# Hybrid encoder step: feed-forward as seven block products for eight, operands made in the attention output's evacuation, rms applied behind the products

## The chip, the cores and the metric

One core of a Trainium2 chip. TensorE (PE) multiplies into PSUM, of which there are eight banks of 128 x 512 words; VectorE (DVE), ScalarE (ACT) and GpSimd (POOL) do the elementwise work, the first two with access to PSUM; SyncE (SP) issues every transfer of this kernel. The metric is the device time of one execution in microseconds, the median of the runs shown.

## What is computed

One layer of an encoder for 1024 prompt tokens and 32 sample tokens, T = 1056 in all, with 1024 features. Two token mixers, a cross-attention to 256 memory rows, then a gated feed-forward of width 2816 and a last norm. The part that the change touches:

```python
x = x + cross_attend(rmsnorm(x, lw['norm_cross']), mk, mv, lw['w_cq'], lw['w_co'])
n = rmsnorm(x, lw['norm_ffn'])
x = x + (jax.nn.silu(n @ lw['w_ff1']) * (n @ lw['w_ff3'])) @ lw['w_ff2']
...
y_prompt = rmsnorm(xp, norm_final)
```

All inputs are float32.

## The kernel before

Activations are kept feature-major: a tile of 128 features by up to 1056 tokens. Every large matrix product is done in the fast float32r form of TensorE, with each operand split into a high and a low part (a ScalarE copy to float32r, then a subtraction), and three products for one: high by high, high by low, low by high. `gemm` runs over token blocks of 352 (`BLOCKS`), for each over the k tiles of 128, with three matmuls per k tile, and hands each filled PSUM bank to an evacuation. `load_w` brings a column tile of a weight, multiplies it by a gain where one is given (VectorE), and splits it.

Nothing is issued as it is written: each call becomes a node of a graph, and `Graph.order` simulates the five engines with prices (`price`), picks for each engine the most urgent node (longest path to the end less a bias), and gives out PSUM banks and SBUF places. The order on each engine is then fixed, the queue of SP included. SBUF is cut into regions (`REGIONS`, in units of 66 words a partition, given out in pages of 16 units): f0 and wr hold float32, r0 float32r, mb and ma change their type from phase to phase. `FIFO` says how many tiles of a class may live at once. `LEAD` says how many nodes of earlier phases may be left when a phase opens.

The last stages are:

- `cross` ends with the product by `w_co`, eight column tiles in three blocks each. Its evacuation `residual` adds the product to x, which is held as its two parts `xh` and `xl`, splits the sum into them again (ScalarE, GpSimd), and gathers the squares; `rstd` makes 1/rms of every token, `rb`.
- `ffn` makes the hidden layer in 22 column tiles of 128. For each, two `gemm` calls over x (`w_ff1`, `w_ff3`, with the gain multiplied into the weights), evacuations `evac1` and `evac3` that apply `rb`, the sigmoid and the gate, and a split of the hidden values into two parts that stay in SBUF. After 6, 12, 18, 20 and 22 hidden tiles (`FF_GROUPS`) `ff2` multiplies a group by its rows of `w_ff2` and adds to eight accumulators `acc`; the residual x is added in the first two groups.
- The last group goes block by block (`LAST`), followed by `final`: transposes to token-major, the last norm, the writes.

## Time and profile before

| | |
|---|---|
| median of 3 runs | 2032.84 us (2032.03 to 2032.9) |
| the profiled execution, first to last instruction | 2034.7 us |
| TensorE, busy | 1954.2 us |
| VectorE, ScalarE, GpSimd, busy | 1101.1, 801.0, 622.5 us |
| mean granted TensorE clock | 0.978 |
| HBM read, written | 86.69, 11.55 MB |

The times in the table but the first row are of one profiled execution. The busy time of an engine is the union of its instructions' spans. PE rows are matmuls, PEld rows weight loads. In the rows of groups, a name before the arrow is what is written and one behind it what is read: `bank` is PSUM, and the other names are the regions of SBUF (r is r0; f is f0), since every instruction is issued from one line of `emit`. Shapes are partitions by elements; the numbers behind the first bar are the group's busy time in us and the mean of one instruction in ns. Lines of the timeline begin with start and length in us; the rows by stretch give busy us and instruction counts of PE, PEld, DVE, ACT and POOL.

### The profile page before, as it was taken

The page shows a single profiled execution, that of the slowest core. Times are in us where ns is not written, and L with a number is a line of the kernel's source. Part 1 is how long each engine was busy: PE and PEld are TensorE (multiplying, and loading weights), DVE is VectorE, ACT ScalarE, POOL GpSimd, SP SyncE. Part 2 cuts the span into 40 slices and gives each one's busy share as a digit, 9 for nine tenths or more (in the row PEclk, how much of TensorE's full clock was granted, in tenths as well). Part 3 has the DMA queues.
Part 4 walks back from the last instruction along what each step waited for, and adds up shares of the span by engine and source line. Part 5 has one row for each costly group of instructions (what it writes and reads, how often), then busy time and mean ns, then how long its engine had stood idle before and what let it go on. Part 6 is the DMA issues. An engine that isn't in the chain of part 4 may idle for free.

```text
span 2034.7 us, 36538 instructions
## 1 busy us (share of the span) xinstructions
PE 1954.2 (96%) x14417; PEld 1813.2 (89%) x14417; DVE 1101.1 (54%) x2584; ACT 801.0 (39%) x2066; POOL 622.5 (31%) x954
## 2 busy tenths in 40 slices
PE   7989999998999899899999999999999999999998
PEld 6878777787877788899989999999999999999997
DVE  4876677768767766635754356333333344323345
ACT  4576546845765676633332233121111112111122
POOL 4742343334434331206300056230022233310221
PEclk8999999998999999899999999999999999999999
DMA  4100100011010101541211111111211111111112
GB/s 139 42 22 25 35 23 27 23 34 33 22 32 18 33 23 58 179 147 42 73 42 42 42 53 42 42 40 40 59 50 39 40 58 42 50 40 53 46 42 86
DMA packets 159115, 100.59 MB, mean 49 GB/s; under 512 B 7776, under 2 KB 153824, under 8 KB 158944
## 3 DMA queue, kind: packets, MB, share of 16 engines
q1 hardware_dynamic: 158944, 98.26, 16.0%
q8 instruction: 113, 1.85, 0.4%
q14 instruction: 58, 0.48, 0.1%
HBM read 86.69 MB, written 11.55 MB: 48 GB/s over the span
## 4 chain that ended last, share of the span: by engine, by line
PE 59%; DVE 4%; POOL 1%; ACT 1%; issue 1%; DMA 1%; SPq 0%; DVEq 0%; ACTq 0%
PE bank L337 59%; DVE f L337 2%; ACT f L337 1%; POOL f L337 1%; DVE r L337 1%; POOL r L337 1%; DVE mb L337 0%; ACT mb L337 0%; DMA wr<-in_w_ck_dram 0%; ACT r L337 0%; DMA f<-mix_scratch 0%; DMA wr<-in_w_cq_dram 0%; DVE wr L337 0%; SPq L337 0%; POOL mb L337 0%
## 5 line engine op out<-in xcount | busy, mean ns | idle before, releaser
L337 PE MATMUL bank<-r 128*128 128x352 f32 x5904 | 1040.1, 331 | 12.4 <-POOL r L337 5.3
L337 PEld LDWEIGHTS bank<-r 128*128 128x128 f32 x5904 | 955.1, 190 | 27.6 <-POOL r L337 5.8
L337 DVE TENSOR_TENSOR f<-bank,f 128x256 f16<-128x256 f32 (+9 forms) x689 | 252.6, 391 | 355.4 <-PE bank L337 339.8
L337 PE MATMUL bank<-mb,r 128*128 128x352 f32 (+3 forms) x2448 | 411.5, 325 | 4.6 <-DVE r L337 2.5
L337 PEld LDWEIGHTS bank<-mb,r 128*128 128x128 f32 x2448 | 396.1, 188 | 9.5 <-DVE r L337 4.3
L337 POOL TENSOR_TENSOR f<-f 128x352 f32<-128x352 f32 (+6 forms) x242 | 198.2, 835 | 482.0 <-ACT f L337 459.4
L337 PE MATMUL bank<-f 128*128 128x64 f16 (+7 forms) x2612 | 291.6, 253 | 35.2 <-DVE f L337 15.7
L337 ACT CAST r<-wr 128x1024 fp32r<-128x1024 f32 (+2 forms) x154 | 145.1, 946 | 311.8 <-PE bank L337 298.1
L337 ACT ACTIVATE f<-f 128x256 f32<-128x256 f32 (+5 forms) x372 | 147.0, 411 | 245.9 <-DVE f L337 217.7
L337 PEld LDWEIGHTS bank<-f 128*128 128x128 f32 (+4 forms) x1564 | 163.6, 162 | 66.8 <-DVE f L337 16.9
L337 ACT COPY f<-f 64x256 f16<-64x256 f16 (+1 forms) x408 | 149.1, 367 | 46.1 <-DVE f L337 37.8
L337 DVE TENSOR_TENSOR r<-wr,r 128x1024 fp32r<-128x1024 f32 (+2 forms) x124 | 142.1, 1150 | 43.5 <-ACT r L337 43.3
L337 DVE TENSOR_TENSOR wr<-wr,f 128x1024 f32<-128x1024 f32 x82 | 105.8, 1292 | 104.5 <-DMA wr<-in_w_ff_dram 89.1
L337 POOL TENSOR_TENSOR r<-f,r 128x352 fp32r<-128x352 f32 x48 | 62.3, 1312 | 271.1 <-DVE f L337 216.9
L337 POOL TENSOR_SCALAR f<-f 128x64 f32<-128x64 f32 (+6 forms) x124 | 54.7, 442 | 159.2 <-DVE f L337 100.0
L337 DVE TENSOR_TENSOR ma<-bank,ma 128x352 f32<-128x352 f32 (+6 forms) x96 | 45.3, 486 | 94.6 <-PE bank L337 84.1
L337 PEld LDWEIGHTS <-f 128*128 128x128 f16 x1156 | 52.5, 99 | 35.6 <-issue 8.2
L337 POOL TENSOR_TENSOR r<-wr,r 128x1024 fp32r<-128x1024 f32 x30 | 71.7, 2393 | 29.5 <-ACT r L337 25.9
L337 ACT CAST mb<-f 128x352 fp32r<-128x352 f32 x66 | 30.9, 484 | 123.0 <-DVE f L337 114.7
L337 PE MATMUL bank<-f,mb 64*64 64x64 f32 (+7 forms) x830 | 75.3, 250 | 1.4 <-DVE f L337 1.1
L337 ACT ACTIVATE f<-bank,f 128x256 f32<-128x256 f32 (+4 forms) x122 | 51.1, 432 | 56.4 <-DVE f L337 19.7
L337 DVE TENSOR_TENSOR f<-bank,r 128x352 f32<-128x352 f32 x60 | 30.4, 518 | 77.0 <-PE bank L337 77.0
(167 smaller groups left out, 1770.6 us busy)
## 6 DMA issues: line engine op xcount, KB each, us to landing
wr<-in_w_ff_dram SPq DMA_DIRECT2D x44, 512.0 KB
wr<-in_w_in_dram SPq DMA_DIRECT2D x30, 512.0 KB
wr<-in_w_ff_dram SPq DMA_DIRECT2D x24, 384.0 KB
f<-mix_scratch SPq DMA_DIRECT2D x24, 176.0 KB
mb<-in_x_prompt_dram SPq DMA_DIRECT2D x16, 256.0 KB
wr<-in_w_ck_dram SPq DMA_DIRECT2D x8, 512.0 KB
wr<-in_w_cv_dram SPq DMA_DIRECT2D x8, 512.0 KB
wr<-in_w_out_dram SPq DMA_DIRECT2D x8, 512.0 KB
```

Source lines behind the costliest of these rows:

```text
L337: getattr(eng, method)(*args, **kw)
```

## The change

The feed-forward's three matrix products are done blockwise, 2 x 2 blocks on each side, with seven block products for eight (Winograd's form of Strassen's scheme). For the hidden layer a block of the weight is 512 inputs by 128 columns and a block of x 512 features by 264 tokens; the token halves are taken twice (`s` = 0, 1), each of 2 x 264 tokens. The weight's sums are made by `fast_w` from a raw tile of 256 columns as they are needed (four sums, then a high and a low part for each of seven operands). The sums of x (`operands`) are made in the evacuation of the product by `w_co`, which now runs in four blocks of 264, scales x by the norm's gain there and writes x itself to a scratch in DRAM. `xh` and `xl` then hold the operands of products 1, 2, 3 and 7; those of 5, 6 and 4 are split in `ff_hidden`. `fast` runs the seven products in a given order into four pairs of banks, three of which are used twice.

`ff_hidden` makes all 11 pairs of hidden tiles first; 1/rms is applied to both factors behind the products in tiles of 4 x 264. The hidden values and their differences are written to DRAM, and `ff_out` reads them back as operands of `w_ff2`, ten pairs in five groups of two, split anew; x is read back and added in the third group, and sums common to several output blocks are added in the last. The eleventh pair is multiplied plainly, block by block as before, with `final` behind it; `final`'s identity is made anew ahead of it. float32r weights have a region of their own, cut from r0. Elsewhere the diff removes comments.

```diff
-FF_GROUPS = (6, 6, 6, 2, 2)
+FF_GROUPS = (2, 2, 2, 2, 2)
+TQ = T // 4
...
-REGIONS = {"f0": (192, "left", "FFFFFF", ()), "wr": (32, "left", "FFFFFF", ()), "r0": (320, "left", "RRRRRR", ()),
-           "mb": (192, "left", "FRRRRR", (150,)), "ma": (64, "right", "FRRRFF", (1000, 150))}
+REGIONS = {"f0": (192, "left", "FFFFFFF", ()), "wr": (32, "left", "FFFFFFF", ()), "r0": (256, "left", "RRRRRRR", ()), "rw": (64, "left", "RRRRRRR", ()),
+           "mb": (192, "left", "FRRRRRR", (150,)), "ma": (64, "right", "FRRRFFF", (1000, 150))}
...
-LEAD = {0: BIG, 1: 1100, 2: 250, 3: 400, 4: 300, 5: 40}    # a phase opens when so many nodes of the ones before it are left
+LEAD = {0: BIG, 1: 1100, 2: 250, 3: 400, 4: 300, 5: 200, 6: 200}
...
+FIFO = {"wr": 2, "wh": 2, "wl": 2, "p": 44, "rp": 5, "op": 56, "sr": 2, "sh": 4, "sl": 4, "sx": 4, "sh3": 8, "sl3": 8, "hst2": 4, "xr": 2, "wr2": 4, "wh2": 8, "wl2": 8, "ckv": 7, "mrow": 2}
...
-            self.gemm(w, act, KD, self.residual(m, sq))
+            self.gemm(w, act, KD, self.operands(m, sq), blocks=[(TQ * q, TQ) for q in range(4)])
...
+    def operands(self, m, sq):
+        nc = self.nc
+        V, S, G = nc.vector, nc.scalar, nc.gpsimd
+        def new(name):
+            return self.ap.tile([128, TQ], F32, tag=name, name=name)
+        def evac(t0, n, ps):
+            s, h = divmod(t0 // TQ, 2)
+            hs, ls = self.xh[:, m, t0:t0 + n], self.xl[:, m, t0:t0 + n]
+            t, x, k = new("xs"), new("xg"), m % 4
+            self.x[m, s, h] = x
+            V.tensor_tensor(t, ps, hs.bitcast(F32), ALU.add)
+            V.tensor_tensor(t, t, ls.bitcast(F32), ALU.add)
+            S.activation(x, t, AF.Copy, scale=self.P("g_ffn", m))
+            nc.sync.dma_start(self.x_dram[:, m, t0:t0 + n], t)
+            if m >= 4 or h == 0:
+                self.split(hs, ls, x)
+            if m < 4 and h == 1:
+                t1 = self.t[5, k, s] = new("t1")
+                G.tensor_tensor(t1, x, self.x[k, s, 0], ALU.subtract)
+            if m >= 4 and h == 1:
+                E = V if m == 7 else G
+                t2, t3, t4 = self.t[6, k, s], _, self.t[4, k, s] = new("t2"), new("t3"), new("t4")
+                E.tensor_tensor(t3, x, self.x[k, s, 1], ALU.subtract)
+                self.split(self.xh[:, k, t0:t0 + n], self.xl[:, k, t0:t0 + n], t3)
+                E.tensor_tensor(t2, x, self.t[5, k, s], ALU.subtract)
+                E.tensor_tensor(t4, self.x[m, s, 0], t2, ALU.subtract)
+            if m == 0:
+                S.activation(sq[:, t0:t0 + n], t, AF.Square)
+            else:
+                S.activation(t, t, AF.Square)
+                G.tensor_tensor(sq[:, t0:t0 + n], sq[:, t0:t0 + n], t, ALU.add)
+        return evac
...
+    def halves(self, ap):
+        v = ap.rearrange("p (s h u) -> p s h u", s=2, h=2)
+        return v[:, :, 0], v[:, :, 1]
...
+    def fast_w(self, ap, nk, order, tags, pairs):
+        nc = self.nc
+        V, S, G = nc.vector, nc.scalar, nc.gpsimd
+        raw = self.wp.tile([128, nk, 2, 256], F32, tag="sr", name="fraw")
+        if pairs:
+            nc.sync.dma_start(raw, ap.rearrange("(k e p) m -> p k e m", e=2, p=128))
+        else:
+            for e in range(2):
+                nc.sync.dma_start(raw[:, :, e], ap[128 * nk * e:128 * nk * (e + 1)].rearrange("(k p) m -> p k m", p=128))
+        a11, a21, a12, a22 = raw[:, :, 0, 0:128], raw[:, :, 0, 128:256], raw[:, :, 1, 0:128], raw[:, :, 1, 128:256]
+        s1, s2 = (self.ap.tile([128, nk, 128], F32, tag="sx", name=t) for t in ("s1", "s2"))
+        G.tensor_tensor(s1, a21, a22, ALU.add)
+        G.tensor_tensor(s2, s1, a11, ALU.subtract)
+        for i in order:
+            if i == 7:
+                G.tensor_tensor(a21, a11, a21, ALU.subtract)
+            if i == 3:
+                G.tensor_tensor(a12, a12, s2, ALU.subtract)
+            part = {1: a11, 2: a12, 3: a12, 4: a22, 5: s1, 6: s2, 7: a21}[i]
+            hi, lo = (self.wp.tile([128, nk, 128], F32R, tag=tag, name="f" + tag[:2]) for tag in tags)
+            S.copy(hi, part)
+            V.tensor_tensor(lo, part, hi.bitcast(F32), ALU.subtract)
+            yield hi, lo
...
+    def fast(self, ws, act, nk, evac, order):
+        nc = self.nc
+        ps = {}
+        for i in order:
+            nc.bias = self.turn
+            self.turn += 0.73 * nk
+            hi, lo = next(ws)
+            bank = " aadcdbc"[i]
+            fresh = (bank, 0) not in ps
+            for s in range(2):
+                if fresh:
+                    ps[bank, s] = self.psg.tile([128, TQ], F32, tag="g", name="ps_f")
+                p = ps[bank, s]
+                for k in range(nk):
+                    if k % CUT == 0:
+                        nc.cut()
+                    ah, al = act(i, k, 0, s), act(i, k, 1, s)
+                    nc.tensor.matmul(p, lhsT=hi[:, k], rhs=ah, start=fresh and k == 0, stop=False, skip_group_check=True)
+                    nc.tensor.matmul(p, lhsT=hi[:, k], rhs=al, start=False, stop=False, skip_group_check=True)
+                    nc.tensor.matmul(p, lhsT=lo[:, k], rhs=ah, start=False, stop=k == nk - 1, skip_group_check=True)
+                evac(i, s, p)
...
+    def ff_hidden(self):
+        nc = self.nc
+        V, S, G = nc.vector, nc.scalar, nc.gpsimd
+        ops = {}
+        self.turn = 0.0
+        for n, i in enumerate((5, 6, 4)):
+            nc.bias = 3.0 * n
+            for k in range(4):
+                for s in range(2):
+                    ops[i, k, s] = [self.ap.tile([128, TQ], F32R, name=f"t{i}{p}") for p in "hl"]
+                    self.split(*ops[i, k, s], self.t[i, k, s])
+        def act(i, k, lo, s):
+            if i in (4, 5, 6):
+                return ops[i, k, s][lo]
+            t0 = TQ * (2 * s + (i in (3, 7)))
+            return (self.xl if lo else self.xh)[:, k + 4 * (i in (2, 3)), t0:t0 + TQ]
+        rb = self.rb.rearrange("p (s h u) -> p s h u", s=2, h=2)
+        dram = []
+        for m in range(DFF // 256):
+            last = m == DFF // 256 - 1
+            shape = [128, 2, T] if last else [128, 2, 7, TQ]
+            d = nc.real.dram_tensor(f"h_scratch{m}", shape, F32, kind="Internal").ap()
+            dram.append(nc.tile(shape, F32, f"h_dram{m}", fixed=d))
+            cs = slice(256 * m, 256 * m + 256)
+            order = (1, 6, 7, 5, 4, 2, 3) if m else (1, 2, 7, 5, 3, 6, 4)
+            out, u, full = [[None, None], [None, None]], [None, None], [False, False]
+            def sums(f, i, s, ps):
+                if i == 1:
+                    out[f][s] = self.ap.tile([128, 4, TQ], F32, tag="ft4", name="tv"[f])
+                    u[s] = self.ap.tile([128, TQ], F32, tag="fu", name="fu")
+                    full[s] = False
+                    S.copy(u[s], ps)
+                    return
+                o = out[f][s]
+                if i == 6:
+                    V.tensor_tensor(u[s], ps, u[s], ALU.add)
+                    full[s] = True
+                    if order[1] != 6:
+                        G.tensor_tensor(o[:, 2], o[:, 2], u[s], ALU.add)
+                        G.tensor_tensor(o[:, 3], o[:, 3], u[s], ALU.add)
+                elif i == 2:
+                    S.copy(o[:, 0], ps)
+                elif i == 5:
+                    V.tensor_tensor(o[:, 2], ps, o[:, 2], ALU.add)
+                else:
+                    dst = o[:, {7: 2, 4: 1, 3: 3}[i]]
+                    if full[s]:
+                        V.tensor_tensor(dst, ps, u[s], ALU.add)
+                    else:
+                        S.copy(dst, ps)
+            def evac1(i, s, ps):
+                sums(0, i, s, ps)
+                if i == order[-1]:
+                    t, sg = out[0][s], self.ap.tile([128, 4, TQ], F32, tag="ft4", name="sg")
+                    r = rb[:, s].unsqueeze(2).to_broadcast([128, 2, 2, TQ])
+                    th = t.rearrange("p (h a) u -> p h a u", a=2)
+                    V.tensor_tensor(th, th, r, ALU.mult)
+                    S.activation(sg, t, AF.Sigmoid)
+                    G.tensor_tensor(t, t, sg, ALU.mult)
+                    (G if s else V).tensor_tensor(th, th, r, ALU.mult)
+            def evac3(i, s, ps):
+                sums(1, i, s, ps)
+                if i == order[-1]:
+                    x, y = out[1][s], self.ap.tile([128, 4, TQ], F32, tag="ft4", name="ht")
+                    V.tensor_tensor(x, x, out[0][s], ALU.mult)
+                    if last:
+                        for b, (e, h) in enumerate(((0, 0), (1, 0), (1, 1), (0, 1))):
+                            t0 = TQ * (2 * s + h)
+                            nc.sync.dma_start(dram[m][:, e, t0:t0 + TQ], x[:, b])
+                        return
+                    G.tensor_tensor(y[:, 2], x[:, 3], x[:, 0], ALU.subtract)
+                    G.tensor_tensor(y[:, 0], x[:, 2], y[:, 2], ALU.subtract)
+                    G.tensor_tensor(y[:, 1], x[:, 2], x[:, 3], ALU.subtract)
+                    G.tensor_tensor(y[:, 3], x[:, 1], y[:, 0], ALU.subtract)
+                    nc.sync.dma_start(dram[m][:, s, 0:3], x[:, 0:3])
+                    nc.sync.dma_start(dram[m][:, s, 3:7], y)
+            for name, evac in (("w_ff1", evac1), ("w_ff3", evac3)):
+                self.fast(self.fast_w(self.i[name][0, :, cs], 4, order, ("sh", "sl"), False), act, 4, evac, order)
+        return dram
...
+    def ff_out(self, hidden):
         V, S, G = nc.vector, nc.scalar, nc.gpsimd
         fp = self.ap
+        order = (1, 6, 7, 5, 2, 4, 3)
+        acc = [fp.tile([128, T], F32, tag="ac", name="acc") for _ in range(KD)]
+        common = [fp.tile([128, 2, TQ], F32, tag="ac", name="common") for _ in range(KD // 2)]
+        def operands(ms):
+            ops = {}
+            for at, i in enumerate(order):
+                nc.bias = self.turn + 0.73 * len(ms) * at
+                for k, m in enumerate(ms):
+                    raw = fp.tile([128, 2, TQ], F32, tag="hst2", name="hraw")
+                    nc.sync.dma_start(raw, hidden[m][:, :, (0, 0, 1, 2, 6, 5, 3, 4)[i]])
+                    hi, lo = (fp.tile([128, 2, TQ], F32R, tag="op", name=t) for t in ("fh", "fl"))
+                    S.copy(hi, raw)
+                    (V if k % 2 else G).tensor_tensor(lo, raw, hi.bitcast(F32), ALU.subtract)
+                    ops[i, k] = hi, lo
+            return lambda i, k, lo, s: ops[i, k][lo][:, s]
+        def evac(g, j, i, s, ps):
+            c = [[h[:, s] for h in self.halves(acc[2 * j + e])] for e in range(2)]
+            dst = {1: common[j][:, s], 6: common[j][:, s], 2: c[0][0], 7: c[1][1], 5: c[1][1], 4: c[1][0], 3: c[0][1]}[i]
+            if g == 0 and i not in (5, 6):
+                S.copy(dst, ps)
+            else:
+                V.tensor_tensor(dst, ps, dst, ALU.add)
+            if i == order[-1] and g == len(FF_GROUPS) - 1:
+                for n, dst in enumerate((c[1][1], c[1][0], c[0][1])):
+                    (V if n == 2 else G).tensor_tensor(dst, dst, common[j][:, s], ALU.add)
+        at = 0
+        for g, n in enumerate(FF_GROUPS):
+            rows = slice(256 * at, 256 * (at + n))
+            act = operands(range(at, at + n))
+            for j in range(4):
+                w = self.fast_w(self.i["w_ff2"][0, rows, 256 * j:256 * j + 256], n, order, ("sh3", "sl3"), True)
+                self.fast(w, act, n, partial(evac, g, j), order)
+                if g == 2:
+                    for m in (2 * j, 2 * j + 1):
+                        x = fp.tile([128, T], F32, tag="xr", name="xr")
+                        nc.sync.dma_start(x, self.x_dram[:, m])
+                        G.tensor_tensor(acc[m], acc[m], x, ALU.add)
+            at += n
+        nc.phase, nc.bias = 6, self.turn
+        hs = []
+        for e in range(2):
+            raw = fp.tile([128, T], F32, tag="xr", name="hraw2")
+            nc.sync.dma_start(raw, hidden[at][:, e])
+            hs.append([fp.tile([128, T], F32R, name=t) for t in ("fh2", "fl2")])
+            self.split(*hs[e], raw, V if e else G)
+        ws = [self.load_w(self.i["w_ff2"][0, 256 * at:, 128 * m:128 * m + 128], 2, small=True) for m in range(KD)]
...
+        for b in LAST:
+            for m in range(KD):
+                def add(t0, n, ps, m=m):
+                    V.tensor_tensor(acc[m][:, t0:t0 + n], ps, acc[m][:, t0:t0 + n], ALU.add)
+                self.gemm(ws[m], lambda k, lo, t0, n: hs[k][lo][:, t0:t0 + n], 2, add, blocks=[b])
```

78 lines of the change are left out of this document (18 added, 60 removed).

## The prediction

> **What bounds the kernel now.** I read the page, then the chain of waits, then the table by stretches.
>
> ```profile
> span 2034.7 us, 36538 instructions
> ...
> PE 1954.2 (96%) x14417; PEld 1813.2 (89%) x14417; DVE 1101.1 (54%) x2584; ACT 801.0 (39%) x2066; POOL 622.5 (31%) x954
> ...
> PEclk8999999998999999899999999999999999999999
> ...
> GB/s 139 42 22 25 35 23 27 23 34 33 22 32 18 33 23 58 179 147 42 73 42 42 42 53 42 42 40 40 59 50 39 40 58 42 50 40 53 46 42 86
> ```
> ```profile
> 1254.16 0.86 PE bank L337 x2
> 1255.05 753.06 PE bank L337 x4654
> 2009.52 0.59 POOL f L337
> ```
> ```profile
> core 0: us, PE busy (x) PEld busy (x) DVE busy (x) ACT busy (x) POOL busy (x), PEclk, DMA share, GB/s
> 1160.00:1230.00 70.00, 69.65 (x429) 69.06 (x429) 27.11 (x39) 18.70 (x37) 30.76 (x27) 1.00 0.13 39
> 1230.00:1260.00 30.00, 28.93 (x169) 27.01 (x169) 23.89 (x31) 13.81 (x27) 23.21 (x18) 1.00 0.19 53
> ...
> 1400.00:1950.00 550.00, 550.00 (x3410) 550.00 (x3409) 197.75 (x288) 88.51 (x141) 124.11 (x114) 1.00 0.16 47
> ```
>
> The chain has one unbroken piece of 753 us in which nothing but TensorE decides: the feed-forward. In the 550 us stretch inside it TensorE never stops, its granted clock is 1.00, and VectorE, ScalarE and GpSimd are busy 36%, 16% and 23%. So this stage's time is the number of products times their spacing: 550 / 3410 = 161.3 ns for a moving operand of 352 columns. Fewer or narrower products are worth their full spacing here, and there is elementwise room to pay with.
>
> **What one narrower product costs.** The change uses moving operands of 264 columns; none runs in this kernel. The nearest row is the memory's keys and values, with 256 columns (timeline, then groups kept apart by shape):
>
> ```profile
> 842.00 5.87 PE L337 MATMUL bank<-r,ma 128*128 128x256 f32 x48
> ```
> ```profile
> L337 PEld LDWEIGHTS bank<-r 128*128 128x128 f32 x5904 | 955.1, 190 | 27.6 <-POOL r L337 5.8 <-ACT mb L337 3.4 <-DVE r L337 2.7
> L337 PE MATMUL bank<-r,ma 128*128 128x256 f32 x384 | 53.2, 296 | 0.9 <-DVE r L337 0.9
> L337 PEld LDWEIGHTS bank<-r,ma 128*128 128x128 f32 x384 | 49.9, 201 | 1.7 <-DVE r L337 1.1 <-ACT r L337 0.2 <-ACT f L337 0.2
> ```
>
> Forty-eight in 5.87 us, the last one's own 296 ns taken off: (5.87 - 0.296) / 47 = 118.6 ns. The line to 161.3 at 352 columns is 0.445 ns a column, so 264 columns cost 118.6 + 8 x 0.445 = 122.2 ns. A weight load lasts about 190 ns by either row, yet one passes every 118.6 ns: loads overlap, and a load's length is no floor at 122.
>
> The Trainium skill (TensorE: Matmul & The Clock Gate, Back-to-back issue gap) gives for back-to-back products one column per 2.4 GHz cycle plus 2.5 ns: 149.2 and 112.5 ns as estimates from that page, and the exchange below would then save 83 us; the trace's spacings are 8 to 9% longer, and I use those.
>
> **Products.** Removed: 22 column tiles x 8 x 3 x 3 blocks for each of two input matrices, and 20 x 8 x 3 x 3 of the output matrix: 4608 x 161.3 ns = 743.3 us (the last pair, 144 products, stays as it is). Added: 11 pairs x 2 x 7 products x 2 halves x 12 = 3696, and 5 groups x 4 x 7 x 2 x 6 = 1680: 5376 x 122.2 ns = 656.9 us. Gain 86.4 us. The attention output is re-cut from 3 blocks to 4: 768 x 122.2 - 576 x 161.3 ns = +0.9 us. Net -85.5 us on the path that sets the end.
>
> **Elementwise work, against 41.1 us of TensorE per unit** (one pair of the hidden layer or one group of the output matrix: 336 x 122.2 ns either way).
>
> ```profile
> L337 POOL TENSOR_TENSOR f<-f 128x352 f32<-128x352 f32 x96 | 104.2, 1111 | 389.8 <-ACT f L337 388.6
> L337 DVE TENSOR_TENSOR f<-bank,f 128x352 f32<-128x352 f32 x114 | 58.8, 523 | 197.6 <-PE bank L337 197.5
> L337 DVE TENSOR_TENSOR r<-wr,r 128x1024 fp32r<-128x1024 f32 x38 | 47.1, 1240 | 12.6 <-ACT r L337 12.6
> L337 DVE TENSOR_TENSOR wr<-wr,f 128x1024 f32<-128x1024 f32 x38 | 46.6, 1226 | 73.2 <-DMA wr<-in_w_ff_dram 73.1
> L337 ACT CAST r<-wr 128x1024 fp32r<-128x1024 f32 x38 | 39.6, 1043 | 51.4 <-PE bank L337 51.4
> ```
> ```profile
> L337 DVE TENSOR_TENSOR r<-wr,r 128x256 fp32r<-128x256 f32 x16 | 6.2, 422 | 0.0
> L337 ACT CAST r<-wr 128x256 fp32r<-128x256 f32 x16 | 6.0, 404 | 4.1 <-DMA wr<-in_w_ff_dram 4.0
> ```
> ```profile
> 1256.52 1.38 DVE L337 TENSOR_SCALAR f<-bank 128x352 f32<-128x352 f32 x3
> ```
> ```profile
> L337 POOL TENSOR_TENSOR r<-wr,r 128x1024 fp32r<-128x1024 f32 x30 | 71.7, 2393 | 29.5 <-ACT r L337 25.9 <-PE bank L337 3.2
> ```
>
> Three VectorE instructions of 352 columns in a row took 1.38 us, the last one about 0.52: they start every 0.43 us. With some 1.07 ns a column between 256 and 1024 columns, VectorE gives 0.32 (256), 0.33 (264), 0.60 (512), 0.62 (528) and 1.2 us (1056). ScalarE, 0.83 ns a column: 0.40, 0.41, 0.62, 0.63, 1.07. GpSimd, 1.11 to 2.39: 0.93, 0.94, 1.42, 1.45, 2.45.
>
> Hidden layer, per pair. VectorE: 14 low parts of 512, 20 sums of 264, 5 multiplies of 1056: 8.4 + 6.6 + 6.0 = 21 us. ScalarE: 14 high parts, 8 copies, 2 sigmoids: 14 us. GpSimd: 8 weight sums, 3 multiplies of 1056, 8 differences: 11.4 + 7.4 + 7.5 = 26 us. All lie beside 41.1 us of products; the 44 multiplies by the gain at about 1.23 us (the wr<-wr,f row) go away. Uncovered, each engine's excess over 41.1 would count.
>
> Output matrix, per group. VectorE: 56 sums of 264, 28 low parts of 256, 7 of 528: 18.5 + 9.0 + 4.3 = 32 us. ScalarE 20 us. GpSimd: 16 weight sums, 7 low parts: 25 us; the third group adds 8 x 2.45 us for the residual, together 44.6, over the 41.1; the last adds 16 x 0.94, together 40.
>
> Now the row that speaks against the change. Where VectorE's two inputs are both SBUF and GpSimd runs, they take turns:
>
> ```profile
> 1235.80 2.42 POOL L337 TENSOR_TENSOR f<-f 128x352 f32<-128x352 f32 x2
> ...
> 1236.14 0.51 DVE L337 TENSOR_TENSOR f<-bank,r 128x352 f32<-128x352 f32 x1
> ...
> 1236.57 2.03 DVE L337 TENSOR_TENSOR f<-f,r 128x352 f32<-128x352 f32 x2
> ...
> 1238.17 1.23 POOL L337 TENSOR_TENSOR r<-f,r 128x352 fp32r<-128x352 f32 x1
> ...
> 1238.52 1.97 DVE L337 TENSOR_TENSOR r<-wr,r 128x1024 fp32r<-128x1024 f32 x1
> ```
>
> Two 352-column adds from SBUF took 2.03 us for 0.95 alone, and a low part 1.97 for 1.24; the add with an input from PSUM, under a running GpSimd, kept its 0.51. So sums out of PSUM are free of GpSimd and the rest adds to it. Added in line, per hidden pair 14.4 + 26 = 40 of 41 us; per output group 13 + 25 = 38, in the third 58, in the last 56 with its combining adds. The first kind just fits and costs delay, not rate. For the third group the price lies between 0 (GpSimd's rows above already hold some waiting, and operands are kept two groups ahead) and 17 us; I take 8, near the middle. For the last, 0 to 15, I take 3, since its combining adds gate only the plain pair. For the other three 0 to 5, I take 1. Hidden layer: 0 to 15 over eleven pairs, I take 3. Output matrix +12, hidden +3.
>
> **Start of the feed-forward.** The 24 operands of products 5, 6 and 4 are split in a region which the attention's operands leave only when its last product has run. In the first call (20.5 us) VectorE then has 24 x 0.33 + 11 low parts x 0.6 + the rms chain and sums, some 25 us, and GpSimd is already late there (23.21 of 30 us). Between 0 (this call's order puts products 6 and 4 last) and 10 (its excess over 20.5, with GpSimd's turns); I take 4. Beside it, each of 32 blocks writes x to DRAM and ScalarE's square, in place, waits for that write; behind it stand the high parts of the next block. ScalarE is busy 18.70 of 70 us in this stage, and even 1 us more a block leaves it under the 94 us of products: nothing, and up to 32 us of ScalarE if that cover were gone.
>
> **Transfers.** The hidden values go out (48 writes) and come back (70 reads of 270 KB and 2 of 540), with 32 + 8 for x. Per output group that is 14 x 0.27 + 4 x 0.52 = 5.9 MB in 41 us, 143 GB/s, against 47 in the stretch above. The page's rate by slices reached 179, so it fits; four buffers give each read some 11 us. All go through SP's one queue, where a write waiting for VectorE holds the weight loads behind it; these are asked for a call, 20 us, ahead. Taken as nothing, kept in the range.
>
> The tail is the same plain pair and final norm, with the identity remade by GpSimd ahead of it; VectorE arrives there busier: +1 (-3 to +4).
>
> **Sum.** The profiled execution: 2034.7 - 85.5 + 3 + 12 + 4 + 1 = 1969.2 us. The runs' median is 1.9 us under that span, so 1967.
>
> **Rivals.**
> 1. All of it hides: only products count. 2034.7 - 85.5 - 1.9 = 1947, 1948 with the tail. For it: the engines' sums above are all under 41.1 but one. Against: the taking of turns. 0.20.
> 2. Taking turns decides the whole output matrix: 35 SBUF-only VectorE instructions a group each wait half a microsecond behind GpSimd, 32 + 17 = 49 us for 41; five groups lose 40, the start 8, the hidden layer 5: 1948 + 53 = 2001. For it: GpSimd's occupancy of 60% and more; against: today's low parts, at 23% GpSimd, take 1240 ns against 1226 for the same-sized multiply, hardly any waiting. 0.20. The Trainium skill (SBUF — State Buffer, Who interferes with whom) states it as an exclusive lock held for a whole instruction; by that rule the trace agrees, 2.03 us for two adds.
> 3. Narrow products don't hold their spacing, as on arrival of freshly made weights: at 138 ns, 5376 x 138 = 742, nothing is gained, the attention output costs 13 more, and with the other terms it is 2034.7 - 1 + 13 + 20 - 1.9 = 2065. Against: the 256-column row. 0.02.
> 4. Slower: room. A pair's sums live in tiles of 16 units, and if the next pair's cannot be given out until this pair's hidden values are written, TensorE stands through the last sum 0.33, multiply 1.2, four differences 3.8 and a write of about 2.7 (an estimate): 8 us x 11 = 88, 1967 + 88 = 2055. It decides from fewer than six free places; I count 16 places of 16 units less two for the raw weights, two for constants, three for weight sums and small tiles, so nine. 0.06.
> 5. My forecast, 1967, own range 1955 to 1985. 0.52.
>
> **How the numbers follow.** A measurement of this kernel tells about 0.2% (4 us) from no change. Forecast, 1 and 2 are all faster: 0.92; of the 0.08 of 3 and 4, milder forms of which end near today's time, 0.01 is put within 0.2% and 0.07 slower. The range takes in rival 1 less 3 us for a planner that orders the earlier stages anew, and rival 2: 1945 to 2004.
>
> **What would show it.** Right: 5376 products with 264 columns at 121 to 123 ns where they run in a row; a chain of TensorE through the hidden layer in 440 to 470 us; the five output groups at 205 to 230 us with gaps of TensorE released by VectorE or GpSimd in the third; low parts of the weights longer than 0.6 and 0.42 us. Wrong: spacing over 130 ns; gaps at each pair's start released by a DMA or by GpSimd; TensorE idle over 40 us in all of the feed-forward.

## The result, and the profile after

| | before | after |
|---|---|---|
| median of the runs compared, us | 2032.43 (2030.44 to 2032.9, 4 runs) | 2044.99 (2041.77 to 2047.24, 4 runs) |
| ratio | 1 | 1.0062 [1.0048, 1.0076] |
| profiled execution's span, us | 2034.7 | 2040.0 |

The change makes the kernel 0.6% slower. 1967 us was forecast, within 1945 to 2004. The page of the changed kernel, with the rows that answer to those shown of the one before:

```profile
span 2040.0 us, 40406 instructions
...
PE 1892.7 (93%) x15377; PEld 1739.6 (85%) x15377; DVE 1431.3 (70%) x3093; ACT 944.9 (46%) x2454; POOL 910.2 (45%) x1159
...
PE   7899999998998999899999997999999999899898
...
PEclk9999989999999999899999998999999999999999
...
PE 8%; DVE 3%; issue 2%; POOL 2%; DMA 1%; ACT 0%; DVEq 0%; ACTq 0%; POOLq 0%
```

TensorE's busy time fell by 61.5 us (1954.2 to 1892.7) and the span rose. The work did leave TensorE; its place was taken by idle time. The unbroken piece of 753 us of TensorE at the end of the chain is gone as well. The feed-forward's stages by stretch (columns: length, then busy us and instructions of PE, PEld, DVE, ACT, POOL, then the granted clock, the DMA share, GB/s): the product by `w_co` and the first pair, the other ten pairs, the output matrix.

```profile
1134.00:1320.00 186.00, 162.90 (x1193) 156.05 (x1192) 126.06 (x218) 80.83 (x194) 85.58 (x77) 0.94 0.20 63
1320.00:1760.00 440.00, 413.15 (x3295) 407.67 (x3294) 311.68 (x384) 126.16 (x240) 272.84 (x193) 0.98 0.30 100
1760.00:1990.00 230.00, 214.19 (x1691) 209.06 (x1691) 219.30 (x418) 100.50 (x251) 145.71 (x133) 0.99 0.44 137
```

In the hidden layer no engine but TensorE is over 71% busy, and TensorE still stands for 27 of 440 us. What ended those stops (the table of waits of that stretch: us in all, times, the longest):

```profile
PE bank L340 <- DVE ma L340: 16.6, 8, 2.9
PE bank L340 <- DVE f L340: 4.7, 2, 2.7
PE bank L340 <- ACT rw L340: 3.8, 8, 1.0
PE bank L340 <- DVE rw L340: 1.7, 8, 0.2
```

A sum of VectorE ("ma", "f") ends the large ones, about one a pair. One of them in the timeline of the changed kernel (start, length, engine, operation, how many, idle time before and who ended it):

```profile
1427.86 0.69 DVE L340 TENSOR_TENSOR rw<-ma,rw 128x512 fp32r<-128x512 f32 x1
...
1428.93 1.26 DVE L340 TENSOR_TENSOR f<-f 128x1056 f32<-128x1056 f32 x1
...
1431.43 2.80 POOL L340 TENSOR_TENSOR f<-f,ma 128x1056 f32<-128x1056 f32 x1 [6.18 <-ACT ma L340]
1431.81 5.85 DVE L340 TENSOR_TENSOR rw<-ma,rw 128x512 fp32r<-128x512 f32 x2
...
1434.18 5.81 POOL L340 TENSOR_TENSOR f<-f 128x1056 f32<-128x1056 f32 x2
...
1437.58 0.76 DVE L340 TENSOR_TENSOR f<-bank,f 128x264 f32<-128x264 f32 x2
...
1438.22 3.10 PE L340 MATMUL bank<-mb,rw 128*128 128x264 f32 x24
1438.27 2.27 DVE L340 TENSOR_TENSOR rw<-ma,rw 128x512 fp32r<-128x512 f32 x1
1439.95 1.73 POOL L340 TENSOR_TENSOR ma<-wr 128x512 f32<-128x512 f32 x1
1440.46 2.33 DVE L340 TENSOR_TENSOR f<-f 128x1056 f32<-128x1056 f32 x1
...
1442.72 0.42 DVE L340 TENSOR_TENSOR ma<-bank,f 128x264 f32<-128x264 f32 x1
...
1443.29 3.19 PE L340 MATMUL bank<-mb,rw 128*128 128x264 f32 x24 [1.97 <-DVE ma L340]
```

The first two rows show VectorE alone: 0.69 us for a low part of 512 columns, 1.26 for a multiply of 1056. GpSimd's three multiplies of the gate (2.80 and 5.81 us) then run from 1431.4 to 1440.0. Under them two low parts take 5.85 us and a third 2.27; a fourth instruction, the multiply, takes 2.33 under GpSimd's weight sum. The sums out of a bank keep about 0.4 us each. VectorE does its queue in order, so the sum at 1442.72, whose bank the next product needs, stands behind them, and TensorE waits 1.97 us. This comes back at the same product of every pair: ten stops of 2.2 to 3.2 us, some 45 us apart. In the 11 us ahead of eight of them VectorE is never idle, and two low parts and a multiply there take 2.3 to 3.0 us each. In the whole stretch VectorE stood 2.0 us for a result of GpSimd, so it is not a link of GpSimd's that is late at these stops, but VectorE's own instructions that last longer.

Grouped by shape, the hidden layer's stretch 1330 to 1760:

```profile
L340 DVE TENSOR_TENSOR rw<-ma,rw 128x512 fp32r<-128x512 f32 x68 | 100.5, 1491 | 13.4 <-ACT rw L340 13.1 <-PE bank L340 0.2
L340 DVE TENSOR_TENSOR f<-f 128x1056 f32<-128x1056 f32 x38 | 64.4, 1694 | 3.5 <-POOL f L340 2.0
L340 DVE TENSOR_TENSOR f<-bank,f 128x264 f32<-128x264 f32 x151 | 62.4, 425 | 37.5 <-PE bank L340 36.4 <-ACT rw L340 0.7
L340 POOL TENSOR_TENSOR f<-f 128x1056 f32<-128x1056 f32 x19 | 54.1, 2869 | 0.0
```

The mean low part takes 1491 ns, more than twice its 690 alone.

**Where the 85.5 us went.** The start of each stage is that of its first product of 264 columns in the timeline; "at pace" is the number of products by the spacing measured where they run in a row, 121.7 ns. The first feed-forward product starts at 1246.6 us before and at 1257.3 after.

| term | predicted, us | measured, us |
|---|---|---|
| products of the feed-forward: 743.3 to 5376 x 121.7 ns = 654.3 | -86.4 | -89.0 |
| start of the first pair, `w_co` in it | +0.9 | +10.7 |
| first pair: 61.9 for 336 at pace, 40.9 | +4 | +21.0 |
| other ten pairs: 449.9 for 3360 at pace, 408.9 | +3 | +41.0 |
| output matrix: 228.2 for 1680 at pace, 204.5 | +12 | +23.7 |
| tail, with what is left over | +1 | -2.1 |
| sum, on 2034.7 | 1969.2 | 2040.0 |

Of the 41.0, 31.0 us are gaps between two products (those of over 0.4 us) and 10.0 a spacing a little over 121.7 (clock 0.98 in that stretch).

### The profile page after: what moved, and what is told of

Read it like the earlier page. It is cut to its first block, busy times and chain, and to the rows that moved or that the text cites. A ratio compares the mean times of both kernels' runs of the same rounds, so it can differ in the third digit from the quotient of the medians.

```text
span 2040.0 us, 40406 instructions
## 1 busy us (share of the span) xinstructions
PE 1892.7 (93%) x15377; PEld 1739.6 (85%) x15377; DVE 1431.3 (70%) x3093; ACT 944.9 (46%) x2454; POOL 910.2 (45%) x1159
## 5 line engine op out<-in xcount | busy, mean ns | idle before, releaser
L340 PE MATMUL bank<-r,rw 128*128 128x264 f32 (+1 forms) x5664 | 914.4, 313 | 32.0 <-DVE rw L340 6.1
L340 PEld LDWEIGHTS bank<-r,rw 128*128 128x128 f32 x5664 | 811.2, 191 | 55.3 <-DVE rw L340 9.0
L340 PE MATMUL bank<-mb,rw 128*128 128x264 f32 (+4 forms) x3600 | 505.0, 296 | 50.0 <-DVE ma L340 19.8
L340 PEld LDWEIGHTS bank<-mb,rw 128*128 128x128 f32 x3600 | 478.1, 192 | 61.5 <-issue 26.0
L340 DVE TENSOR_TENSOR f<-bank,f 128x264 f32<-128x264 f32 (+6 forms) x895 | 321.6, 384 | 163.3 <-PE bank L340 148.5
L340 POOL TENSOR_TENSOR f<-f 128x264 f32<-128x264 f32 (+8 forms) x255 | 240.0, 954 | 303.6 <-ACT f L340 237.9
L340 PE MATMUL bank<-f 128*128 128x64 f16 (+6 forms) x2630 | 297.4, 253 | 35.8 <-DVE f L340 16.1
L340 ACT CAST rw<-wr 128x256 fp32r<-128x256 f32 (+2 forms) x223 | 145.5, 660 | 298.1 <-PE bank L340 171.3
L340 DVE TENSOR_TENSOR rw<-wr,rw 128x256 fp32r<-128x256 f32 (+2 forms) x193 | 178.5, 928 | 68.5 <-ACT rw L340 63.3
L340 ACT ACTIVATE f<-f 128x256 f32<-128x256 f32 (+7 forms) x374 | 151.4, 422 | 111.5 <-DVE f L340 89.9
L340 DVE TENSOR_TENSOR f<-f 128x256 f32<-128x256 f32 (+8 forms) x152 | 115.2, 773 | 27.9 <-ACT f L340 14.8
L340 ACT ACTIVATE f<-bank,f 128x256 f32<-128x256 f32 (+4 forms) x122 | 51.0, 431 | 61.9 <-DVE f L340 26.1
```

Of the source, the lines that this page charges most:

```text
L340: getattr(eng, method)(*args, **kw)
```

## The experiments

Two theories stood at the outset. **Turns:** GpSimd's instructions that read SBUF hold up VectorE's with two SBUF inputs, and through VectorE's queue the sums that free a bank. **Rivals:** GpSimd is merely a link of a chain that is too long; VectorE or ScalarE has too much to do; the order of the instructions is bad by itself. The stages of every run, in us of its profiled execution, counted as above (a run of the changed kernel's plan has `w_co` at about 123, most of those with another plan between 112 and 118). Executions of one and the same kernel lie 5 to 13 us apart, so a few us in one stage of one profiled execution prove nothing by themselves.

| run | `w_co` | first pair | ten pairs | output | median, us | ratio to before |
|---|---|---|---|---|---|---|
| the change | 122.7 | 61.9 | 449.9 | 228.2 | 2044.99 | 1.0062 [1.0048, 1.0076] |
| multiplies on VectorE | 112.2 | 69.9 | 461.3 | 224.5 | 2048.38 | 1.0076 [1.0052, 1.01] |
| Silu | 122.8 | 56.6 | 416.3 | 228.1 | 2002.56 | 0.9847 [0.982, 0.9874] |
| quarters | 114.1 | 63.3 | 446.5 | 226.5 | 2031.13 | 0.9988 [0.9976, 0.9999] |
| square apart | 123.4 | 58.5 | 451.4 | 235.2 | 2042.96 | 1.0047 [1.0031, 1.0063] |
| planner with turns | 114.8 | 64.4 | 443.1 | 237.9 | 2038.7 | 1.0028 [1.0014, 1.0042] |
| Silu and planner | 114.9 | 62.1 | 408.6 | 229.3 | 1993.61 | 0.9809 [0.9786, 0.9833] |
| Silu and GpSimd writes | 134.3 | 64.1 | 426.7 | 228.7 | 2033.04 | 1.0 [0.9987, 1.0013] |
| no squares | 118.0 | 54.0 | 448.0 | 232.2 | 2029.34 | 0.9979 [0.9966, 0.9993] |
| Silu on the kernel before | | | | | 2033.13 | 1.0 [0.9989, 1.0011] |
| x into the sums | 122.1 | 62.0 | 441.4 | 229.4 | 2036.38 | 1.0018 [1.0006, 1.003] |
| Silu, planner, low parts | 114.9 | 63.4 | 408.5 | 225.0 | 1990.04 | 0.9787 [0.9773, 0.98] |
| and the residual moved | 114.3 | 63.6 | 408.7 | 218.3 | 1984.5 | 0.9755 [0.974, 0.977] |
| start with less GpSimd | 115.7 | 49.7 | 452.8 | 230.4 | 2033.7 | 1.001 [0.9996, 1.0025] |
| start with less VectorE | 115.2 | 61.1 | 446.7 | 233.4 | 2038.0 | 1.0032 [1.0015, 1.0049] |

### The gate's multiplies: moved to VectorE, or gone

```diff
-                    G.tensor_tensor(t, t, sg, ALU.mult)
-                    (G if s else V).tensor_tensor(th, th, r, ALU.mult)
+                    V.tensor_tensor(t, t, sg, ALU.mult)
+                    V.tensor_tensor(th, th, r, ALU.mult)
```

> The 33 hidden-layer multiplies of 4 x 264 that GpSimd does (22 by the sigmoid, 11 by 1/rms; 2.8 to 2.9 us each in the changed kernel's trace) go to VectorE. Taking turns (GpSimd's long instructions hold up VectorE's SBUF-only ones): VectorE gains 33 x 1.25 = 41 us of work, but loses its waits; the low parts of 512 fall from 1491 ns towards 700, TensorE's idle time in the hidden layer (27 us of 430) halves, 2020 to 2032 us. Rival, VectorE simply has too much work: the hidden layer grows by up to 41 us, 2055 to 2085 us.

Measured 2048.38 us, over the range that turns gave and under the rival's; the ten pairs take 461.3. VectorE's low parts did fall, to a mean of 687 ns (1330 to 1740), but nothing is gained by handing the reads to VectorE. The waits of the hidden layer in this run (1320 to 1760):

```profile
PE bank L340 <- DVE rw L340: 30.6, 9, 3.5
```

The stop is now at the low parts of the weights ("rw"), 3.5 us once a pair, behind VectorE's own multiplies of 1056 columns. The Trainium skill (Perfetto Trace Analysis, Optimizing Scalar/DVE Operations) says that moving work between these two engines might not help; this run agrees.

The second edit takes the multiply away: one Silu of ScalarE for a sigmoid and a multiply by it, 22 of 2.9 us in all.

```diff
-                    S.activation(sg, t, AF.Sigmoid)
-                    G.tensor_tensor(t, t, sg, ALU.mult)
+                    S.activation(t, t, AF.Silu)
```

> ScalarE's Silu takes the place of its sigmoid and of GpSimd's multiply by it: 22 x 2.87 = 63 us of GpSimd go, nothing is added. Taking turns: the hidden layer's TensorE idle time falls by a third to a half, 2022 to 2035 us. Rival, VectorE's amount of work: VectorE has as much as before, no change, 2040 to 2048 us.

Measured 2002.56 us, better than either range: 63 us less of GpSimd's reads brought 42 us. The ten pairs fall by 33.6 us, and there is hardly a stop left in them (up to their last): the waits of 1320 to 1715, then the low parts of 1320 to 1720.

```profile
PE bank L340 <- DVE rw L340: 0.4, 1, 0.4
```
```profile
L340 DVE TENSOR_TENSOR rw<-ma,rw 128x512 fp32r<-128x512 f32 x70 | 73.9, 1059 | 31.5 <-ACT rw L340 31.4
```

### Is it the Silu by itself?

On the kernel before, the same exchange takes away 96 multiplies of 352 columns.

> The kernel before with one Silu on ScalarE in place of a sigmoid on ScalarE and a multiply on GpSimd (96 multiplies of 352 columns, 104.2 us of GpSimd). Taking turns: in the kernel before TensorE was never late in the feed-forward, so GpSimd's reads cost nothing there, and the same edit that gave the changed kernel 42 us gives this one nothing: 2029 to 2037 us. Rival (the Silu is worth its 42 us by itself, by a shorter chain or by less load on the chip's clock): 1990 to 2015.

Measured 2033.13 us, ratio 1.0. The stretch of the prediction again:

```profile
1400.00:1950.00 550.00, 550.00 (x3410) 550.00 (x3409) 197.73 (x286) 88.98 (x142) 79.16 (x70) 1.00 0.16 47
```

GpSimd's busy time in it went from 124.11 to 79.16 us and TensorE's products did not move. The Silu is worth something only where VectorE is late for TensorE. The rival falls.

### Reading, or being busy?

Silu again, and in place of each multiply five writes of a constant into a tile of the same size, which read nothing (`G.memset(sg, 0.0)`, five times).

> The Silu form, and in the place of each removed multiply GpSimd fills a tile of 4 x 264 with zeros five times (about 3 us that read nothing). If GpSimd's reading of SBUF is what holds VectorE up: as the Silu form, 1997 to 2010 us. If GpSimd's being busy or late is the cause: back to the changed kernel, 2035 to 2048 us.

The total, 2033.04 us, is 30 us over Silu's alone and in neither range. The writes wait for no input, so the planner put them where it liked: of the 110, 69 run between 1134 and 1320 us, 41 in the 63 us behind it and none later. In the third to tenth pair the gaps are 0.0 to 0.4 us, as with Silu alone, but no write stands there. So the time of the stages does not answer the question. Single instructions do (1340 to 1370):

```profile
1345.56 8.36 POOL L340 MEMSET f<- 128x1056 f32 x9
1345.64 1.26 DVE L340 TENSOR_TENSOR f<-f 128x1056 f32<-128x1056 f32 x1 [0.30 <-POOL f L340]
...
1347.16 0.68 DVE L340 TENSOR_TENSOR rw<-wr,rw 128x512 fp32r<-128x512 f32 x1
...
1361.01 0.62 ACT L340 CAST rw<-wr 128x512 fp32r<-128x512 f32 x1 [18.84 <-POOL wr L340]
1361.65 0.69 DVE L340 TENSOR_TENSOR rw<-wr,rw 128x512 fp32r<-128x512 f32 x1 [9.86 <-ACT rw L340]
```

Under a row of writes VectorE's multiply and low part keep the 1.26 and 0.68 us that they take alone. From 1134 to 2000 us, 23 low parts of 512 columns that overlap writes only have a mean of 685 ns, 64 that overlap nothing 687, and 64 that overlap GpSimd instructions that read 1300. What lengthens VectorE's instructions is GpSimd's reading, not its being busy. The Trainium skill (SBUF — State Buffer, Who interferes with whom) gives it as a lock held for a whole instruction, for VectorE's two SBUF inputs only against a GpSimd instruction that reads SBUF; these rows agree.

The 30 us have another cause: 11.5 in `w_co`, 7.5 in the first pair and 12 in the second, where the writes stand. GpSimd's own sums come late behind them. In the last rows ScalarE waits 18.84 us for one sum of the weights, and VectorE 9.86 for ScalarE. TensorE's stops that end at such a high part ("ACT rw") come to 22.9 us between 1138 and 1380, against 5.0 with Silu alone between 1135 and 1358. So a late GpSimd costs time as well, where it has more to do than fits. In the ten pairs of the changed kernel the stops that end at the weights' parts ("ACT rw", "DVE rw") are 5.5 of 26.8 us.

### Shorter instructions

The same multiplies on GpSimd, each as four of 264 columns, so that a turn is shorter.

> The same 33 multiplies stay on GpSimd, each as four of 264. Same elements, so GpSimd's total stays (four starts for one, about 0.1 us each more). If what hurts is how long VectorE is held at a time: a wait is at most 0.9 us in place of 2.9, 2025 to 2037 us. If it is the sum of both engines' work on what they share, nothing is gained: 2042 to 2052 us.

Measured 2031.13 us, within the range of the theory that the length of a turn decides. But the ten pairs got only 3.4 us shorter; most of the gain is `w_co`, 8.6 us, where nothing was edited and where the planner made another order. VectorE's multiplies in 1330 to 1730, and what ended TensorE's stops in 1320 to 1760:

```profile
L340 DVE TENSOR_TENSOR f<-f 128x1056 f32<-128x1056 f32 x45 | 65.7, 1462 | 21.6 <-POOL f L340 19.8
```
```profile
PE bank L340 <- DVE rw L340: 10.6, 10, 3.7
PE bank L340 <- ACT rw L340: 9.0, 8, 1.8
PE bank L340 <- DVE f L340: 6.6, 8, 1.3
```

VectorE's instructions lose less to turns (multiplies 1462 ns for 1694, low parts 1079 for 1491), and the stops at its sums shrink from 21.3 us to 6.6. But GpSimd is now late: its instructions of 264 columns take 935 ns each, four of them 3.7 us for 2.9, VectorE stands 19.8 us for its results, and 19.6 us of TensorE's stops end at the weights' parts. The loss has moved and not gone. The Trainium skill (Perfetto Trace Analysis, Optimizing Scalar/DVE Operations) holds that breaking instructions up may help where an engine with room to spare leaves bubbles on others; here it hardly did.

### Is the order at fault?

The planner's simulation does not know of turns. The edit (the core of it) tells it, from phase 3 on, for VectorE's instructions with two SBUF inputs and GpSimd's with one or more:

```diff
+                    if n.port:
+                        s = max(s, port["gpsimd" if e == "vector" else "vector"])
...
+            if n.port:
+                port[e] = clock[e]
```

> Work unchanged; from the cross-attention on, the planner that orders the queues is told that a VectorE instruction with two SBUF inputs and a GpSimd instruction that reads SBUF exclude each other. Its own forecast rises from 1701 to 1775 (before, without this rule: 1774). Taking turns as the cause of the loss: the sums that free banks stand ahead of what would be held up, TensorE's 2 to 3 us per pair shrink to about 2, 2025 to 2042 us. Rival, the amount of work decides and no order helps: 2040 to 2050 us.

Measured 2038.7 us: 6 less than the change, and still 0.3% above before; the range of turns takes it in, the rival's begins at 2040. `w_co` won 8 us, the ten pairs 7, the output matrix lost 10. In the ten pairs the stops at VectorE's sums, which the edit was to avoid, fell from 21.3 us to 2.1, and those at the weights' parts rose from 5.5 to 18.4 (1320 to 1760). This order doesn't make room for the reads; it moves the wait. With Silu, though, there is room to use:

> The Silu form with that planner. Taking turns: what is left of the loss is at the start and in the output matrix (15 + 16 + 23 us over the products' time); a third of it goes, 1980 to 1998 us. Rival: as the Silu form alone, 1997 to 2007 us.

Measured 1993.61 us. The ten pairs take 408.6 us, which is the pace of the products (408.9): there is no gap in them.

### The start

> The square of x in the attention output's evacuation goes to a tile of its own, so ScalarE no longer waits until the write of x has read the tile. Theory that ScalarE's in-order wait makes the start of the feed-forward slow (23 us of TensorE idle between 1160 and 1330 us): 10 to 20 us less, 2025 to 2035 us. Taking turns as the cause there too: no change, 2040 to 2048 us.

The edit gives the squares a tile of their own, so that ScalarE needn't wait until the write of x has read the old one. 2042.96 us; `w_co` 123.4, with the first pair 2.7 us less than in the change, where 10 to 20 were expected. The wait is hidden, as predicted, and this theory of the start falls.

> Leaves out the sum of squares over the features (GpSimd, 28 adds of 264, some 0.95 us each) in the attention output's evacuation, so 1/rms is wrong. Attention output to the first product of the feed-forward takes 122.7 us in the changed kernel, 94 by the products. Taking turns there: 8 to 18 us of it go, 2025 to 2036 us. Rival, ScalarE's waits or weights that arrive late: unchanged, 2040 to 2048 us.

Left out are GpSimd's 28 sums of squares. 2029.34 us: `w_co` and the first pair together 12.6 us shorter, the ten pairs 1.9 shorter, the output matrix 4.0 longer. Part of the 12.6 may be the plan's: runs whose edit does not touch `w_co` have 177 to 185 us for the two stages together (leaving out the run with the writes); this one has 172.0.

Two further runs take away what each engine reads there. The first:

> The changed kernel; left out: GpSimd's part of the sums of x in the evacuation by w_co (26 subtractions, the operands of products 4 to 7 are then plain blocks of x but for the last feature tile) and its 28 additions of squares (1/rms is wrong). Some 53 us of GpSimd with two SBUF inputs go from the start, VectorE and ScalarE keep all their work. The planner, without turns, gives 2 us more than for the changed kernel. Taking turns makes the start late: w_co with the first pair, 184.6 us in the changed kernel against 135 of products, falls by 20 to 35 us, the rest stays: 2010 to 2026. Rival (VectorE's and ScalarE's own work is what is late there, or the clock): it falls by the 13 us of the run without squares or less, 2028 to 2045.

`w_co` and the first pair fall from 184.6 to 165.4 us, 19.2; a little less than turns gave, more than the 13 of the rival, and 12 us under any run that leaves `w_co` as it is. The total, 2033.7, is in the rival's range, since the stages ahead end 8.5 us later in this plan (the first product of `w_co` at 1143.2 us, 1134.7 in the change); the theories differ over the start, and there it is nearer to turns. VectorE's rows of 1134 to 1320, the changed kernel, then this run:

```profile
L340 DVE TENSOR_TENSOR r<-f,r 128x264 fp32r<-128x264 f32 x32 | 26.1, 856 | 1.5 <-ACT r L340 1.5
...
L340 DVE TENSOR_TENSOR mb<-f,mb 128x264 fp32r<-128x264 f32 x24 | 15.7, 703 | 0.0
L340 DVE TENSOR_TENSOR f<-bank,r 128x264 f32<-128x264 f32 x32 | 13.5, 425 | 34.9 <-PE bank L340 34.9
```
```profile
...
L340 DVE TENSOR_TENSOR f<-bank,r 128x264 f32<-128x264 f32 x32 | 13.7, 428 | 22.4 <-PE bank L340 22.1
L340 DVE TENSOR_TENSOR r<-f,r 128x264 fp32r<-128x264 f32 x32 | 13.3, 427 | 4.6 <-ACT r L340 4.6
...
L340 DVE TENSOR_TENSOR mb<-f,mb 128x264 fp32r<-128x264 f32 x24 | 8.8, 422 | 0.1
```

The two kinds of low part shrink from 856 and 703 ns to 427 and 422, and the sum out of a bank stays at 425: 20 us of VectorE's time here was waiting for GpSimd. Whether TensorE's 19.2 us come from that or from GpSimd being late with its sums, as in the run with the writes, this run does not separate: the edit takes away both.

> The changed kernel; left out: VectorE's second addition in the evacuation by w_co (32 instructions of 264 columns from SBUF, 16.4 us; x then lacks its low part). GpSimd keeps all. Taking turns, VectorE's queue is what is held up, so 16 us less in it bring 8 to 18 us at the start: 2026 to 2037. Rival (VectorE has room, 118 of 170 us busy, and only GpSimd or ScalarE is late): 2040 to 2048.

8.3 us off `w_co` and the first pair, 2038.0 us in all: the low end of what turns gave for the start, a microsecond over its range in the total. It is no proof, though: 7.5 of the 8.3 are in `w_co`, and its 115.2 us are also reached by plans without an edit there (112.2 to 114.9). So what VectorE's own queue costs at the start stays open. Over the products' pace, 134.4 us for 1104, the two stages lose 50.2 us in the changed kernel; leaving out GpSimd's work brings back 19 of them, part of which may again be the plan's.

### The output matrix, and the best version

> The changed kernel with x read from DRAM straight into the accumulators ahead of the first output group, whose blocks are then all added: GpSimd's eight residual adds of 1056 columns in the third group (some 21 us of reads) go, VectorE gets six additions of a bank instead of six copies out of one. Taking turns: the third group's stall of 8.6 us falls to the 1 to 5 us of its neighbours and nothing else moves: 2033 to 2043. Rival (the third group is late for another reason, the reads of the hidden values): the group keeps its 8 us, 2041 to 2049.

The edit drops the third group's residual adds by reading x into the accumulators ahead of the first. The third group's gaps fell from 7.5 to 3.9 us, as expected, but those of the first two rose from 6.8 to 11.2, and the stage stayed at 229.4. The total, 2036.38, is 8.6 us under the change's; in the profiled executions that difference lies in the ten pairs, which the edit does not touch, with 2 us less of gaps and a granted clock of 1.00 against 0.98:

```profile
1320.00:1760.00 440.00, 415.36 (x3351) 409.20 (x3351) 309.65 (x394) 130.92 (x249) 270.25 (x194) 1.00 0.31 105
```

So it is no proof for the residual: the delay moved to the groups next to it.

Two more edits, on the version with Silu and turns. First all low parts of the output matrix's operands on VectorE:

```diff
-                    (V if k % 2 else G).tensor_tensor(lo, raw, hi.bitcast(F32), ALU.subtract)
+                    V.tensor_tensor(lo, raw, hi.bitcast(F32), ALU.subtract)
```

> The version with Silu and with the planner told of the turns, and all low parts of the output matrix's operands on VectorE instead of every second one on GpSimd in the first pair's and combining operands. Taking turns: fewer two-input reads of GpSimd, more work on VectorE, whose row was 95% busy in the output stage; the planner with turns gives 5 us less than without the edit: 1984 to 1995. Rival (VectorE's load decides the output stage): its 229 us there become 235 to 245, in all 1995 to 2010.

1990.04 us, within the range of turns; the stage 225.0 for 229.3. Then the residual in the first group, on VectorE (`if g == 0`, and `V` for `G`):

> The same with the residual x added in the first output group and by VectorE, instead of in the third and by GpSimd. Taking turns: eight GpSimd instructions of 1056 columns with two SBUF inputs leave the output stage, VectorE gets eight of about 1.2 us; by the planner with turns 8 us less than the version with Silu and turns alone: 1980 to 1992. Rival (VectorE's load decides): 1995 to 2010.

1984.5 us, within 1980 to 1992, the best of all runs and 2.4% under the kernel before. The rows of its hidden layer and its output matrix, and of VectorE's low parts in the second:

```profile
1320.00:1760.00 440.00, 440.00 (x3620) 440.00 (x3619) 312.92 (x453) 153.60 (x316) 237.63 (x184) 1.00 0.35 116
1725.70:1944.00 218.30, 208.61 (x1682) 205.54 (x1681) 201.11 (x458) 98.00 (x244) 83.34 (x96) 1.00 0.47 147
```
```profile
L340 DVE TENSOR_TENSOR rw<-wr,rw 128x256 fp32r<-128x256 f32 x90 | 42.1, 476 | 1.2 <-PE bank L340 0.6 <-ACT rw L340 0.3 <-issue 0.2
```

The output matrix of the changed kernel, and the same low parts in it:

```profile
1769.20:1997.40 228.20, 211.66 (x1681) 206.34 (x1680) 217.50 (x420) 96.23 (x241) 141.29 (x130) 1.00 0.44 136
```
```profile
L340 DVE TENSOR_TENSOR rw<-wr,rw 128x256 fp32r<-128x256 f32 x92 | 71.2, 779 | 5.0 <-ACT rw L340 4.2 <-PE bank L340 0.7
```

VectorE has more instructions (458 for 420) and is less busy (201.11 us for 217.50): part of what it was busy with was waiting.

## Why the prediction was wrong

**The pace of narrow products: right.** 122.2 ns predicted from the 256-column row, 121.7 measured, so 89.0 us for 86.4; rival 3 never came near.

**The engines' work: right in the main.** Per hidden pair GpSimd was put at 26 us; it was busy 28.3 (282.6 us in the ten pairs), and its rows, too, hold some waiting: a sum of 512 columns takes 1.29 us where no two-input instruction of VectorE runs beside it, and 1.48 in the mean. The low parts did grow beyond 0.6 us, as stated.

**The step that failed: "The first kind just fits and costs delay, not rate", and its price "Hidden layer: 0 to 15 over eleven pairs, I take 3".** The sum held: with what each instruction takes alone (VectorE 0.69 and 1.26 us; GpSimd 1.29, 0.76 and, by one instruction of the run with the planner told of turns, 2.47) a pair comes to 15.9 + 23.8 = 39.7 us. But a sum of loads bounds the delay only if the waits may fall anywhere. VectorE's queue has a place in each pair where four long instructions come ahead of the sum that frees a bank, and GpSimd's three multiplies are due at that very time, since the gate comes out of the same product. The price is a wait per pair and not per layer: 3.1 us of gaps in each of ten, 31.0, with the slower spacing 41.0, where 3 was taken and 15 was the bound. With 40 of 41 us taken there was also no slack in which to place the reads otherwise: in the runs with quarters and with the planner told of turns (446.5 and 443.1 us) the stops at VectorE's sums nearly go, and about as much comes back at the weights' parts. Silu, which takes away about 6 of the 26 us a pair, brings it to 416.3, and with the planner to 408.6.

**The start, 4 predicted, 10 the bound: 32 measured** (10.7 + 21.0, the 0.9 for the narrower products among them; 4.9 stood in the sum). It was worked out for the first call alone. GpSimd's differences and squares run through all of `w_co`, and the low parts beside them took up to twice their time (856 and 703 ns for 427 and 422). How much of the 32 is turns and how much a late GpSimd, the runs don't separate. "ScalarE's wait for the write: nothing" was right.

**The output matrix, 12 predicted: 23.7,** within the ends given for its groups, 0 to 37 in all. The third group was the worst, as said, with 7.5 us of gaps; but the other four have 12.1 together, where 4 was taken.

**Transfers, nothing: right** by what the waits show; no stop of TensorE in the hidden layer ends at a transfer, at 100 GB/s, and 137 in the output matrix. GpSimd did wait for weights in the hidden layer (31.6 us at one of its kinds of sums); whether that adds to the small stops at the weights' parts was not separated.

**The rivals.** Rival 2 named the mechanism and put it in the wrong stage: 40 us in the output matrix, 5 in the hidden layer and 8 at the start, where these stages lost 24, 41 and 32, not all of it to turns. Its evidence against, that low parts take 1240 ns with GpSimd at 23%, said nothing of GpSimd at 62%. Rival 4 (room for tiles) had the sign, not the cause. The chance of "slower" was set at 0.07 with only rivals 3 and 4 behind it; the taking of turns, which had its rows in the trace before, was never carried to a slower end, though the upper ends of its own bounds (15 hidden, 37 output, 10 start, 4 tail) come to 1967 + 46 = 2013, and the hidden layer's 41 in place of its bound of 15 would have made that 2039.

**What stays open.** About 10 us of the ten pairs' loss in the profiled execution is a spacing above 121.7 ns. Most of it lies in four stretches, 17 us in all, in which the granted clock is 0.50; each begins within 1.5 us of the end of a stop of 2.2 to 3.2 us. One of them, behind the stop that ends at 1576.0 us:

```profile
1576.00:1578.00 2.00, 1.99 (x9) 2.00 (x10) 0.89 (x3) 0.07 (x1) 1.89 (x2) 0.50 0.00 0
```

Six other stops of 2.2 us are not followed by a lower clock, and the run with x in the sums has 1.00 throughout with 2 us less of gaps and 3.5 us of slower spacing, so this part changes from run to run. Why `w_co` has 123 us in one plan and 115 in another, without an edit there, was not followed up.

## What to carry to other kernels

Where two engines take turns at one resource, price the turns at the instruction that gates the bottleneck: list what stands ahead of it in its engine's queue and what the other engine does at that time, and multiply by the number of times that this place comes round; a sum of loads that just fits is a warning. Count as a cost of an edit not only elementwise time but reads of SBUF by GpSimd, and look for operations that make them vanish (one activation for a sigmoid and a multiply) before moving them to the other engine: that gained nothing in the hidden layer (461.3 us for 449.9), and 11 us in the output matrix (218.3 for 229.3) once the hidden layer had room. A scheme with fewer products on the bound engine pays only as far as every gap that it opens stays closed: 89 us of products saved brought nothing until 63 us of reads were gone, and 30 to 48 us after that.

## What the runs showed of the hardware

- VectorE with two SBUF inputs under a GpSimd instruction that reads: a low part of 512 columns takes 690 ns alone and 2.27 to 2.9 us under a multiply of 2.8 us or more; beside GpSimd's writes of a constant alone it takes 685. A sum of 264 columns with one input from PSUM keeps a mean of 422 to 427 ns in every run of the changed kernel and its variants.
- More busy time does not mean more work: in the output matrix VectorE's busy time fell from 217.50 us in the changed kernel to 201.11 in the best version, while its instructions rose from 420 to 458.
- TensorE's granted clock was lower at the start of the feed-forward in the changed kernel and its variants, where TensorE also stops. The stretch 1200 to 1300 us, before, the change, and the best version:

```profile
1200.00:1300.00 100.00, 98.58 (x598) 96.07 (x597) 55.02 (x76) 31.90 (x58) 52.53 (x44) 1.00 0.15 43
```
```profile
1200.00:1300.00 100.00, 80.56 (x574) 76.96 (x574) 82.11 (x131) 51.76 (x124) 58.97 (x55) 0.90 0.22 70
```
```profile
1200.00:1300.00 100.00, 81.94 (x582) 77.36 (x581) 69.37 (x129) 49.51 (x121) 50.74 (x53) 0.86 0.23 70
```

A clock of 1.00 became 0.90 and 0.86, in a stage where TensorE was busy 99, 81 and 82 us of 100. The narrow products by themselves are not the reason: the best version's ten pairs run at 1.00 without a stop. In this stretch the variant that stops least, the start with less GpSimd, has 0.96 at 91 us busy, and the one that stops most, the run with the writes, 0.81 at 72. Of the 50.2 us that `w_co` and the first pair lose over the products' pace in the changed kernel, 40 are gaps of over 0.4 us; a slower spacing can be at most the other 10.
